# The S5 scan tile with sequence ahead of group, and x stored earlier through the Pool queue

## The chip, the cores and the metric

The kernel runs on one core of one Trainium2 chip. The metric is the device time of one execution in microseconds, as the median of several runs. The core has TensorE (PE, with its weight loads listed as PEld), VectorE (DVE), ScalarE (ACT), GpSimd (POOL) and SyncE (SP), which here only issues DMAs. ACT and POOL issue DMAs too, each in the order of its own program.

## What is computed

One inference step of a two-layer backbone for 128 prompt tokens and 128 sample tokens, D = 2048, all in float32. Layer 0 has attention, layer 1 an S5 state-space mixer; each is followed by a gated FFN. The change touches layer 1's mixer:

```python
def s5_mixer(h, h0_re, h0_im, w_in, a_re, a_im, log_dt, b_re, b_im, c_re, c_im, d_skip, w_gate, w_out):
    u = f32(h @ w_in)
    ug = u.reshape(bsz, length, N_GROUPS, GROUP_CH)          # 128 groups of 16 channels
    y = f32(d_skip) * u
    for d, rev in ((0, False), (1, True)):
        y_d, s_re, s_im = s5_direction(ug, ...)               # complex linear recurrence, 64 states a group
        y = y + y_d.reshape(bsz, length, D_MODEL)
    y = jax.nn.gelu(y).astype(h.dtype)
    y = y * jax.nn.sigmoid(y @ w_gate)
    return y @ w_out, ...
```

The kernel runs the recurrence over blocks of four positions: 32 steps in place of 128, forward on partitions 0 to 63 and backward on 64 to 127.

## The kernel before

The program is one long list of weight steps. Each loads 512 KB units into eight `raw` buffers (SP issues those loads in order, as buffers come free). Dense products are made from two float32r halves: for each unit ACT writes `whi` (L259 is the helper that records every ACT, DVE and POOL operation), DVE writes `wlo`, and PE runs 12 matmuls of 512 columns. L348 is the helper of all matmuls, L361 that of transposes. Beside the list run background tasks (generators); `pump` lets them emit their next piece when a planner, `Timeline`, thinks that its inputs are ready. The planner's costs (class `Timeline`, `engine`) thus set the order in which the engines' instructions are written; once written, each engine runs its own in order.

The mixer is worked in four quarters q of 32 groups, each in two halves e2 of 16:

- `w_in`: 32 units of dense products (8 for each q), whose result DVE transposes to `u(q)`. Layer norm tiles A6 to A9 are its left operand.
- `scan_task`: ACT masks `u` into `um` (two operations); PE multiplies it with a table into PSUM tiles `ms` (three banks in turn); ACT evacuates each 128x512 result in two halves of 64 partitions into the scan tile `SC` (16 operations of 64x512 for a quarter). The even quarters use tile S0, the odd ones tile X, which is also the tile that holds the activations x. So x is saved to DRAM (`xd`) first and read back at the end of the mixer.
- `steps_task`: the scan, 32 steps of four DVE operations of 128x128 on `SC`.
- `out_task`: ACT copies `SC` into two tiles `sf` (the layout copies, 64x2048, two for each e2); for each e2 PE runs 48 small matmuls (96 passes, in a trace 128x64) whose weights are slices of `sf` or of `u`; ACT applies gelu, PE transposes, ACT writes y. ACT also issues the loads of the next tables here: `cad` (CA, 1 MB) and four pieces `ld` (K, 128 KB each).
- `w_gate`: for each q 32 products of y(q) with raw weights (two passes of 512 columns each), which PE can only begin once y(q) is there. Quarter 3 is a dense product.

`SC` of quarter q + 2 reuses the tile of quarter q, and is written only after the layout copies of q have read it. In `SC`, element order is step, real/imaginary, group, batch: `[P, 33, 2, 32, 2]`. An evacuation and a layout copy then go through it with a distance of 128 elements (512 B) from one element to the next. The planner counts such an ACT operation as 2.15 times as long per element.

Of the kernel before, what the change touches and what calls it, by code (L numbers as in the profile page):

```python
# [11 lines left out]
AF = mybir.ActivationFunctionType  # L12
# [4 lines left out]
P = 128  # L17
# [52 lines left out]
class Timeline:  # L70
# [144 lines left out]
    def engine(self, eng, name, outs, ins, args, kw):  # L215
# [4 lines left out]
        if eng == "ACT":  # L220
            ps = self.in_psum(big[0])
            slow = 1.0
            for x in outs + big:
                st = [d for d in list(x.ap)[1:] if d[1] > 1]
                if st and abs(st[-1][0]) > 16: slow = 2.15
            c = (0.05 if ps else 0.095) + slow * n / 1200.0 + 0.09 * scal + 0.09 * ("accum_out" in kw)
            table = self.SETS.get(args[2], 0)
            if table and table != self.table:
                c, self.table = c + 1.29, table
        elif eng == "POOL":  # L230
            if name == "memset": c = 0.04 + n / 1200.0
# [57 lines left out]
def hybrid_kernel(ctx: ExitStack, tc: tile.TileContext, a):  # L289
# [1056 lines left out]
    class S5:  # L1346
# [25 lines left out]
        def u(self, q):  # L1372
            return self.uy[q // 2][:, q % 2]

        def load_T(self, e, h):
            (act_ if e else sync).dma_start(self.tT[:, h], Td[e][:, h])
# [13 lines left out]
        def scan_task(self):  # L1390
# [7 lines left out]
            self.kt = sb("A10", [P, 2048])  # L1398
            w1 = view(wt, 0, [[64, 2], [2, 32], [1, 2]])
            w2 = view(wt, 128, [[64, 2], [2, 32], [1, 2]])  # L1400
            for q in range(4):
                while not self.u_ready[q]:
                    yield
                while q > 1 and not self.sc_free[q - 2]:
                    yield
                if q == 1:
                    self.xd = dt("xd", [P, 2, D])
                    for b in range(2):
                        sync.dma_start(self.xd[:, b], x[b])
                um = sb("A2", [P, 16, 2, 2, 32])  # L1410
                SC = self.SC[q] = sb(("S0", "X")[q % 2], [P, 33, 2, 32, 2])
                u = self.u(q).rearrange("p (r n) -> p r n", n=64)
                for par in range(2):
                    act(um[:, :, par].rearrange("p r b c -> p r (b c)"), u, AF.Copy, scale=mask_par[:, par:par + 1])
                gps.memset(SC[:, 0, :, :, 0], 0.0)
                gps.tensor_copy(SC[:, 0, :, :, 1], s5par["H0"][:, :, 32 * q:32 * q + 32])
                for e2 in range(2):
                    e = 2 * q + e2
                    for h in range(2):
                        for ri in range(2):  # L1420
                            yield ready(um, tT[:, h], lag=S5_LAG, ahead=AHEAD)
                            bk = ms()
                            for i in range(4):
                                pr = e2 * 8 + h * 4 + i
                                mm(bk[:, i * P:(i + 1) * P], tT[:, h, i, ri],
                                   um[:, pr].rearrange("p a b c -> p (a b c)"), start=True, stop=True)
                            src = bk.rearrange("p (g c) -> p g c", c=32)
                            g0 = (e2 * 16 + h * 8) * 2
                            fw = view(SC, 128 + ri * 64 + g0, [[1, 16], [128, 32]], (0, 64))
                            bw = view(SC, 32 * 128 + ri * 64 + g0, [[1, 16], [-128, 32]], (64, 64))  # L1430
                            act(fw, src[0:64], AF.Copy)
# [3 lines left out]
                while self.scanned < q - 1:  # L1435
                    yield
                a_re = view(s5par["A4"], 32 * q, [[0, 2], [1, 32], [0, 2]])
                a_im = view(s5par["A4"], G + 32 * q, [[G, 2], [1, 32], [0, 2]])
                yield written(SC, lag=S5_LAG, ahead=AHEAD)
                self.scans.append((SC, a_re, a_im, w1, w2, q))  # L1440

        def steps_task(self):
            q = 0
            while q < 4:
# [3 lines left out]
                for s in range(32):  # L1448
                    cur = SC[:, s]
                    swp = view(SC, s * 128 + 64, [[-64, 2], [2, 32], [1, 2]])  # L1450
                    nxt = SC[:, s + 1]
# [9 lines left out]
        def out_task(self):  # L1461
# [8 lines left out]
            for q in range(4):  # L1470
# [4 lines left out]
                if q == 0:  # L1475
                    fin = view(sb("cw", [P, 4, 86]), 0, [[G, 2], [1, G]])
                gps.tensor_copy(fin[:, :, 32 * q:32 * q + 32], SC[:, 32, :, :, 0])
                sfs = [sb(t, [P, 2, 32, 32]) for t in ("A5", "A12")]
                for e2, sf in enumerate(sfs):
                    g0 = e2 * 32  # L1480
                    yield written(SC, lag=S5_LAG, ahead=AHEAD)
                    act(sf[0:64], view(SC, g0, [[64, 2], [1, 32], [128, 32]], (0, 64)), AF.Copy)
                    yield lambda now: tl.t["ACT"] < now + 2.0
                    act(sf[64:128], view(SC, 31 * 128 + g0, [[64, 2], [1, 32], [-128, 32]], (64, 64)), AF.Copy)
                self.sc_free[q] = True
                for e2, sf in enumerate(sfs):
# [3 lines left out]
                    for s in range(8):  # L1490
                        for ph in range(3):
                            for h in range(2):
                                g = h * 8 + s
                                o = bk[64 * h:64 * h + 64, 64 * s:64 * s + 64]
                                if ph < 2:
                                    mm(o, sf[:, ph, 2 * g:2 * g + 2].rearrange("p b c -> p (b c)"),
                                       ca[e % 2][:, g // 8, ph, :, g % 8], start=ph == 0, stop=False,
# [151 lines left out]
    s5 = S5()  # L1649
    m = s5.w_in()  # L1650
    start_hook(ffn0.last_up, lambda: (spawn(s5.steps_task()), spawn(s5.scan_task()), spawn(s5.out_task())))
    held, g1 = fill[-20:-16], fill[-16:]
# [109 lines left out]
```

## Time and profile before

| | us |
|---|---|
| median of three runs (lowest, highest) | 2644.32 (2640.66, 2646.99) |
| profiled execution, its own time | 2647.6 |
| its span | 2645.8 |
| PE busy in it | 2545.2 (96%) |
| DVE, ACT, POOL busy | 1599.1, 1323.0, 442.5 |

The profiled execution is 3.3 us above the median. The mixer lies between 1415 and 1900 us of the span; `w_in` ends at 1553, the dense part of `w_gate` begins at 1725. Most of the kernel is PE at work without a pause. In the stretch of the scans it is not: there PE has pauses of 2 to 14 us, and after them a lower granted clock.

### The profile page before, as it was taken

How to read it: one execution, taken by the hardware profiler on the slowest of the kernel's cores; microseconds unless marked ns; L12 is line 12 of the kernel's file. 1: busy time of each engine (PE TensorE's matmuls, PEld its weight loads, DVE VectorE, ACT ScalarE, POOL GpSimd, SP SyncE). 2: the span in 40 equal slices, each digit the busy share in tenths (PEclk: the TensorE clock that was granted, in tenths of full speed). 3: DMA queues.
4: the chain of work that ended last, by engine and by line, in shares of the span. 5: the costliest groups of instructions: out<-in, count | busy, mean ns of one | idle time of the engine just before them, and what ended most of it. 6: DMA issues, size and time to landing. Idle time of an engine off the chain costs nothing.

```text
span 2645.8 us, 35232 instructions
## 1 busy us (share of the span) xinstructions
PE 2545.2 (96%) x13011; PEld 1893.5 (72%) x13011; DVE 1599.1 (60%) x2370; ACT 1323.0 (50%) x1764; POOL 442.5 (17%) x455
## 2 busy tenths in 40 slices
PE   8999999999999999999998769999999999999998
PEld 4666677667777777777776655466677788888896
DVE  4765554567665665566656386655656565666566
ACT  5333444356554554455455668543555544554354
POOL 0002000011465555455530000000000000000000
PEclk9999999999999999999999889999999999999999
DMA  9979877977888888888886756789677756665663
GB/s 360 321 254 312 295 229 274 365 247 238 263 262 270 272 264 271 263 264 259 275 280 224 220 165 175 218 284 308 221 249 242 242 192 193 186 184 190 191 194 125
DMA packets 388741, 651.11 MB, mean 246 GB/s; under 512 B 81740, under 2 KB 100300, under 8 KB 386648
## 3 DMA queue, kind: packets, MB, share of 16 engines
q1 hardware_dynamic: 364064, 621.10, 71.5%
q10 hardware_dynamic: 20424, 20.47, 3.0%
q0 software_dynamic: 4080, 7.28, 0.9%
q8 instruction: 102, 1.67, 0.3%
q14 instruction: 71, 0.58, 0.1%
HBM read 623.72 MB, written 25.03 MB: 245 GB/s over the span
## 4 chain that ended last, share of the span: by engine, by line
PE 86%; ACT 4%; DVE 4%; DMA 3%; issue 1%; ACTq 1%; POOL 1%; SPq 0%
PE acc L348 73%; PE ada L348 6%; PE ms L361 4%; PE ms L348 3%; ACT A L259 2%; DVE A L259 2%; DVE wlo L259 1%; DMA raw<-in_ada_w_dram 1%; ACT X L259 1%; ACTq L259 1%; ACT whi L259 1%; DMA raw<-in_na_w_o_dram 1%; POOL S L259 1%; ACT S L259 0%; DMA xd<-X 0%
## 5 line engine op out<-in xcount | busy, mean ns | idle before, releaser
L348 PE MATMUL acc<-whi,A 128*128 128x512 f32 (+1 forms) x5536 | 1796.7, 396 | 31.2 <-ACT whi L259 22.4
L259 DVE TENSOR_TENSOR wlo<-raw,whi 128x1024 fp32r<-128x1024 f32 (+2 forms) x697 | 885.8, 1276 | 688.5 <-ACT whi L259 668.8
L348 PEld LDWEIGHTS acc<-whi,A 128*128 128x128 f32 x5536 | 1042.8, 189 | 358.6 <-issue 92.5
L348 PE MATMUL acc<-wlo,A 128*128 128x512 f32 (+1 forms) x2768 | 1080.6, 390 | 11.4 <-DVE wlo L259 10.9
L259 ACT ACTIVATE whi<-raw 128x1024 fp32r<-128x1024 f32 (+2 forms) x697 | 724.5, 1043 | 693.2 <-PE acc L348 557.5
L348 PEld LDWEIGHTS acc<-wlo,A 128*128 128x128 f32 x2768 | 523.2, 189 | 117.7 <-DVE wlo L259 21.0
L259 DVE SCALAR_TENSOR_TENSOR A<-ms,cw,A 128x254 f32<-128x254 f32 x344 | 157.8, 479 | 88.9 <-ACT A L259 80.6
L348 PE MATMUL ada<-raw,cond 128*32 128x512 f32 (+1 forms) x1396 | 196.9, 595 | 6.1 <-DVE adaev L259 4.0
L259 POOL TENSOR_TENSOR S<-S,A 128x512 f32<-128x512 f32 x128 | 182.8, 1448 | 50.3 <-PE ms L361 50.3
L259 POOL DMA_DIRECT2D adab<-in_ada_b_dram x48 | 24.9, 518 | 711.5 <-DVE ada L259 383.6
L259 POOL TENSOR_TENSOR S<-S 128x512 f32<-128x512 f32 (+1 forms) x96 | 132.9, 1384 | 7.5
L259 ACT ACTIVATE A<-ms,cw 128x256 f32<-128x256 f32 x172 | 88.0, 562 | 87.9 <-PE ms L361 87.9
L361 PEld LDWEIGHTS ms<-ident,A 128*128 128x128 f32 (+2 forms) x670 | 80.5, 142 | 47.4 <-ACT A L259 16.2
L361 PE MATMUL ms<-ident,A 128*128 128x128 f32 (+2 forms) x670 | 101.5, 277 | 11.0 <-ACT A L259 10.1
L259 ACT ACTIVATE A<-A 128x512 fp32r<-128x512 f32 (+7 forms) x88 | 72.1, 824 | 66.1 <-DVE A L259 65.5
L259 ACT ACTIVATE A<-ms 128x512 f32<-128x512 f32 (+3 forms) x106 | 55.1, 558 | 96.1 <-PE ms L348 51.0
L348 PE MATMUL ms<-A,A 128*64 128x64 f32 (+1 forms) x1152 | 79.7, 253 | 23.4 <-ACT A L259 19.6
L348 PEld LDWEIGHTS ms<-A,A 128*64 128x64 f32 (+1 forms) x1152 | 75.8, 168 | 35.8 <-ACT A L259 24.2
L259 ACT ACTIVATE S<-ms 128x128 f32<-128x128 f32 (+2 forms) x96 | 58.4, 644 | 70.2 <-PE ms L361 64.5
L348 PE MATMUL acc<-raw,A 128*128 128x512 f32 x192 | 89.3, 614 | 4.3 <-ACT A L259 4.3
L259 ACT ACTIVATE A<-acc 128x512 f32<-128x512 f32 (+1 forms) x112 | 65.2, 588 | 50.4 <-PE acc L348 50.3
L259 POOL DMA_DIRECT2D A<-in_final_g_dram x1 | 0.6, 555 | 504.4 <-ACT whi L259 504.4
(138 smaller groups left out, 1499.0 us busy)
## 6 DMA issues: line engine op xcount, KB each, us to landing
raw<-in_ada_w_dram SPq DMA_DIRECT2D x331, 512.0 KB
raw<-in_ffn_w_up_dram SPq DMA_DIRECT2D x318, 512.0 KB
raw<-in_ffn_w_down_dram SPq DMA_DIRECT2D x168, 512.0 KB
raw<-in_na_w_qkv_dram SPq DMA_DIRECT2D x71, 512.0 KB
raw<-in_s_w_in_dram SPq DMA_DIRECT2D x32, 512.0 KB
raw<-in_s_w_gate_dram SPq DMA_DIRECT2D x32, 512.0 KB
raw<-in_s_w_out_dram SPq DMA_DIRECT2D x32, 512.0 KB
raw<-in_na_w_o_dram SPq DMA_DIRECT2D x28, 512.0 KB
```

Of the source, the lines that this page charges most:

```text
L259: return fn(*args, **kw)
L348: nc.tensor.matmul(out, lhsT, rhs, **kw)
L361: nc.tensor.transpose(out, in_, ident[:n, :n])
```

## The change

Five things are edited:

1. `SC` becomes `[P, 33, 2, 2, 32]`: step, real/imaginary, batch, group. The scan's views follow; its operations stay 128x128.
2. An evacuation writes runs of 8 adjacent elements and reads PSUM with a distance of 64 elements; there are still 16 of 64x512 for a quarter.
3. A layout copy becomes two of 64x1024, each read and written in runs of 8. The tile `sf` gets group innermost, 8 wide, so the weights of 32 of the 48 small matmuls are now read with a distance of 8 elements (32 B).
4. x is stored to DRAM by POOL at the second step of `w_in`, not by SP ahead of quarter 1.
5. The planner no longer counts a distance in PSUM as slow. With this and the shorter runs its orders change on all engines; a pause between the two halves of a layout copy is dropped.

```diff
-                if st and abs(st[-1][0]) > 16: slow = 2.15
+                if st and abs(st[-1][0]) > 16 and not self.in_psum(x): slow = 2.15
...
+        def keep_x(self):
+            self.xd = dt("xd", [P, 2, D])
+            for b in range(2):
+                gps.dma_start(self.xd[:, b], x[b])
...
-                if q == 1:
-                    self.xd = dt("xd", [P, 2, D])
-                    for b in range(2):
-                        sync.dma_start(self.xd[:, b], x[b])
...
-                SC = self.SC[q] = sb(("S0", "X")[q % 2], [P, 33, 2, 32, 2])
+                SC = self.SC[q] = sb(("S0", "X")[q % 2], [P, 33, 2, 2, 32])
...
-                            src = bk.rearrange("p (g c) -> p g c", c=32)
-                            g0 = (e2 * 16 + h * 8) * 2
-                            fw = view(SC, 128 + ri * 64 + g0, [[1, 16], [128, 32]], (0, 64))
-                            bw = view(SC, 32 * 128 + ri * 64 + g0, [[1, 16], [-128, 32]], (64, 64))
+                            src = bk.rearrange("p (g b c) -> p c b g", b=2, c=32)
+                            g0 = e2 * 16 + h * 8
+                            fw = view(SC, 128 + ri * 64 + g0, [[128, 32], [32, 2], [1, 8]], (0, 64))
+                            bw = view(SC, 32 * 128 + ri * 64 + g0, [[-128, 32], [32, 2], [1, 8]], (64, 64))
...
-                sfs = [sb(t, [P, 2, 32, 32]) for t in ("A5", "A12")]
+                sfs = [sb(t, [P, 2, 2, 64, 8]) for t in ("A5", "A12")]
...
-                    act(sf[0:64], view(SC, g0, [[64, 2], [1, 32], [128, 32]], (0, 64)), AF.Copy)
-                    yield lambda now: tl.t["ACT"] < now + 2.0
-                    act(sf[64:128], view(SC, 31 * 128 + g0, [[64, 2], [1, 32], [-128, 32]], (64, 64)), AF.Copy)
+                    for h in range(2):
+                        g0 = e2 * 16 + h * 8
+                        to = sf[:, h].rearrange("p i (b c) g -> p i b c g", b=2)
+                        act(to[0:64], view(SC, g0, [[64, 2], [32, 2], [128, 32], [1, 8]], (0, 64)), AF.Copy)
+                        act(to[64:128], view(SC, 31 * 128 + g0, [[64, 2], [32, 2], [-128, 32], [1, 8]], (64, 64)), AF.Copy)
...
-                                    mm(o, sf[:, ph, 2 * g:2 * g + 2].rearrange("p b c -> p (b c)"),
+                                    mm(o, sf[:, h, ph, :, s],
...
+    start_hook(m[1], s5.keep_x)
```

On DVE, at the end of `w_in`, the order before is as follows (`S_2131` is quarter 0's scan tile, the pair of transposes is `w_in`'s last).

```order
L259 TENSOR_TENSOR wlo_12675<-raw_12420,whi_12674 128x1024
...
L259 TENSOR_TENSOR A_2128_12042<-S_2131_12045,A4t_4707 128x128 x2
L259 TENSOR_TENSOR S_2131_12045<-S_2131_12045,A_2128_12042 128x128 x2
L259 STREAM_TRANSPOSE A_2127_12033<-acc_2209_12548 128x16x32
L259 STREAM_TRANSPOSE A_2127_12033<-acc_2210_12549 128x16x32
L259 TENSOR_TENSOR A_2128_12042<-S_2131_12045,A4t_4707 128x128 x2
L259 TENSOR_TENSOR S_2131_12045<-S_2131_12045,A_2128_12042 128x128 x2
```

After, in the same place (`X_12268` is quarter 1's scan tile):

```order
L259 TENSOR_TENSOR wlo_12697<-raw_12465,whi_12696 128x1024
L259 TENSOR_TENSOR wlo_12715<-raw_12514,whi_12714 128x1024
L259 TENSOR_TENSOR A_2128_12045<-X_12268,A4t_4707 128x128 x2
L259 TENSOR_TENSOR X_12268<-X_12268,A_2128_12045 128x128 x2
...
L259 STREAM_TRANSPOSE A_2127_12036<-acc_2209_12592 128x16x32
L259 STREAM_TRANSPOSE A_2127_12036<-acc_2210_12593 128x16x32
L259 TENSOR_TENSOR A_2128_12045<-X_12268,A4t_4707 128x128 x2
```

Before, five of quarter 0's 32 steps stand behind the last transposes, and its scan begins two `wlo` after the second pair of transposes; now it begins right behind that pair, all 32 steps stand ahead of the last two `wlo`, and seven steps of quarter 1 ahead of the last transposes.

On ACT, behind `w_in`'s last `whi`, before (`A_2230` and `A_2231` are the tiles `sf`, `A_2234` is `um` of quarter 2):

```order
L259 ACTIVATE whi_12674<-raw_12420 128x1024
L259 DMA A_2226_12746<-cad_125 128x2048
L259 ACTIVATE A_2230_12771<-S_2131_12045 64x2048 x2
L259 ACTIVATE A_2231_12772<-S_2131_12045 64x2048 x2
L259 ACT_TABLE_LOAD
L259 ACTIVATE A_2128_12042<-ms_12833 128x8x4x16
...
L259 DMA A_2129_12043<-ld_135 32x16x64 x4
L259 ACTIVATE A_2126_12032<-ms_12987 128x256 x2
L259 ACTIVATE S_2235_12902<-ms_12994 64x16x32 x2
```

And after (`A_2231` is now `um`):

```order
L259 ACTIVATE whi_12714<-raw_12514 128x1024
L259 DMA A_2226_12790<-cad_125 128x2048
L259 ACTIVATE A_2228_12794<-S_2131_12048 64x1024 x4
L259 ACTIVATE A_2229_12795<-S_2131_12048 64x1024 x4
L259 ACTIVATE A_2231_12813<-A_2127_12036,maskpar_70 128x16x64 x2
...
L259 DMA A_2129_12046<-ld_135 32x16x64 x4
L259 ACTIVATE S_2232_12814<-ms_12975 64x32x2x8 x2
L259 ACTIVATE S_2232_12814<-ms_12982 64x32x2x8 x2
L259 DMA A_1939_10985<-td_121 128x1024
L259 ACTIVATE A_2126_12035<-ms_12990 128x256 x2
```

The load of `cad` still stands ahead of the layout copies; `um` of quarter 2 has moved ahead of the gelu, and four evacuations of quarter 2 ahead of the first y.

On POOL the two stores of x stand ahead of quarter 0's first scan writes, with nothing between the last bias loads and them:

```order
L259 DMA adab_80<-in_ada_b_dram 2x512 x2
L259 DMA xd<-X_89 128x2048 x2
L259 MEMSET S_2131_12048 128x2x32
L259 COPY S_2131_12048<-H_942_4708 128x2x32
L259 MEMSET X_12268 128x2x32
```

Before, SP had them between the eleventh and the twelfth of the last sixteen `w_in` loads. On PE, the list of matmuls is the same; ahead of the small matmuls of quarter 1 stand 20 of quarter 0's 32 gate products where there were 32, ahead of those of quarter 2 stand 42 gate products in all where there were 56, and ahead of those of quarter 3 there are 72 where there were 90.

## Rows read from the trace of the kernel before

**Rows 1.** The page's first part: busy us (share of the span), instructions.

```profile
PE 2545.2 (96%) x13011; PEld 1893.5 (72%) x13011; DVE 1599.1 (60%) x2370; ACT 1323.0 (50%) x1764; POOL 442.5 (17%) x455
```

**Rows 2.** Busy us by engine in a slice, then granted clock, DMA share, GB/s.

```profile
1560.00:1580.00 20.00, 8.54 (x180) 8.41 (x182) 18.73 (x77) 18.86 (x8) 0.70 (x3) 0.61 0.36 91
```

**Rows 3.** Timeline of PE: start, us, instruction, count, [idle before <- what ended it].

```profile
1512.75 0.80 PE L348 MATMUL acc<-whi,A 128*128 128x512 f32 x1 [6.84 <-ACT whi L259]
...
1568.53 4.71 PE L348 MATMUL ms<-A,A 128*64 128x64 f32 x96 [14.17 <-ACT A L259]
...
1585.62 3.27 PE L348 MATMUL acc<-raw,A 128*128 128x512 f32 x4
...
1602.96 17.33 PE L348 MATMUL acc<-raw,A 128*128 128x512 f32 x40
...
1665.66 3.02 PE L348 MATMUL ms<-A,A 128*64 128x64 f32 x96
...
1685.06 12.19 PE L348 MATMUL acc<-raw,A 128*128 128x512 f32 x24 [4.34 <-ACT A L259]
```

**Rows 4.** Timeline of ACT (ACTq: DMAs that it issues), same columns.

```profile
1415.83 2.94 ACT L259 ACTIVATE whi<-raw 128x1024 fp32r<-128x1024 f32 x3
...
1430.52 1.04 ACT L259 ACTIVATE whi<-raw 128x1024 fp32r<-128x1024 f32 x1
...
1505.43 1.03 ACT L259 ACTIVATE X<-ms 64x512 f32<-64x512 f32 x1 [7.89 <-DMA xd<-X]
...
1553.41 0.33 ACTq L259 DMA_DIRECT2D A<-cad  x1
1561.03 15.09 ACT L259 ACTIVATE A<-S 64x2048 f32<-64x2048 f32 x4 [15.99 <-DVE S L259]
...
1580.95 3.42 ACTq L259 DMA_DIRECT2D A<-ld  x4
...
1674.06 10.52 ACTq L259 DMA_DIRECT2D A<-ld  x4
```

**Rows 5.** Timeline of DVE, same columns.

```profile
1492.11 1.31 DVE L259 STREAM_TRANSPOSE A<-acc 128x512 f32<-128x512 f32 x2
...
1561.91 0.49 DVE L259 TENSOR_TENSOR A<-X,A4t 128x128 f32<-128x128 f32 x2
...
1595.63 0.53 DVE L259 TENSOR_TENSOR A<-S,A4t 128x128 f32<-128x128 f32 x2
1610.93 0.62 DVE L259 TENSOR_TENSOR S<-S,A 128x128 f32<-128x128 f32 x2 [14.76 <-ACT S L259]
```

**Rows 6.** ACT's groups by shape: count | busy us, mean ns of one | idle.

```profile
L259 ACT ACTIVATE A<-acc 128x512 f32<-128x512 f32 x104 | 61.4, 596 | 48.4 <-PE acc L348 48.3
...
L259 ACT ACTIVATE X<-ms 64x512 f32<-64x512 f32 x32 | 33.9, 1059 | 19.8 <-PE ms L348 7.9 <-DMA xd<-X 7.9 <-issue 3.6
L259 ACT ACTIVATE S<-S 64x384 f32<-64x384 f32 x64 | 33.0, 516 | 5.0 <-POOL S L259 4.6
...
L259 ACT ACTIVATE A<-S 64x2048 f32<-64x2048 f32 x8 | 30.2, 3780 | 16.1 <-DVE S L259 16.0
...
L259 ACT ACTIVATE A<-A 128x1024 f32<-128x1024 f32 x20 | 21.1, 1054 | 5.1 <-DVE A L259 5.1
...
L259 ACT ACTIVATE A<-ms 128x256 f32<-128x256 f32 x16 | 5.2, 383 | 16.0 <-DMA A<-ld 10.4 <-issue 3.2 <-PE ms L361 1.5
```

**Rows 7.** Chain of work that ended last: start, us, what; prices of PE's pieces.

```profile
1480.87 2.76 PE acc L348 x12
1483.63 1.78 PE ms L348 x16
```

**Rows 8.** Groups by shape, 1440 to 1760 us: `wlo`, and PEld's small weights.

```profile
L259 DVE TENSOR_TENSOR wlo<-raw,whi 128x1024 fp32r<-128x1024 f32 x35 | 42.2, 1221 | 63.8 <-ACT whi L259 56.8 <-DMA A<-td 6.8
...
L348 PEld LDWEIGHTS ms<-A,A 128*64 128x64 f32 x768 | 26.1, 152 | 24.2 <-ACT A L259 21.2 <-issue 2.3 <-ACT whi L259 0.8
```

**Rows 9.** The slice (columns as rows 2) in which x becomes final.

```profile
1415.00:1425.00 10.00, 7.27 (x32) 5.78 (x33) 7.74 (x13) 6.32 (x11) 0.00 (x0) 0.83 1.01 360
```

More of the change, by code (lines that the diff above doesn't have):

```diff
@@ L1398, in scan_task @@
             self.kt = sb("A10", [P, 2048])
-            w1 = view(wt, 0, [[64, 2], [2, 32], [1, 2]])
-            w2 = view(wt, 128, [[64, 2], [2, 32], [1, 2]])
+            w1 = view(wt, 0, [[64, 2], [32, 2], [1, 32]])
+            w2 = view(wt, 128, [[64, 2], [32, 2], [1, 32]])
             for q in range(4):
@@ L1414, in scan_task @@
                     act(um[:, :, par].rearrange("p r b c -> p r (b c)"), u, AF.Copy, scale=mask_par[:, par:par + 1])
-                gps.memset(SC[:, 0, :, :, 0], 0.0)
-                gps.tensor_copy(SC[:, 0, :, :, 1], s5par["H0"][:, :, 32 * q:32 * q + 32])
+                gps.memset(SC[:, 0, :, 0], 0.0)
+                gps.tensor_copy(SC[:, 0, :, 1], s5par["H0"][:, :, 32 * q:32 * q + 32])
                 for e2 in range(2):
@@ L1436, in scan_task @@
                     yield
-                a_re = view(s5par["A4"], 32 * q, [[0, 2], [1, 32], [0, 2]])
-                a_im = view(s5par["A4"], G + 32 * q, [[G, 2], [1, 32], [0, 2]])
+                a_re = view(s5par["A4"], 32 * q, [[0, 2], [0, 2], [1, 32]])
+                a_im = view(s5par["A4"], G + 32 * q, [[G, 2], [0, 2], [1, 32]])
                 yield written(SC, lag=S5_LAG, ahead=AHEAD)
@@ L1449, in steps_task @@
                     cur = SC[:, s]
-                    swp = view(SC, s * 128 + 64, [[-64, 2], [2, 32], [1, 2]])
+                    swp = view(SC, s * 128 + 64, [[-64, 2], [32, 2], [1, 32]])
                     nxt = SC[:, s + 1]
@@ L1476, in out_task @@
                     fin = view(sb("cw", [P, 4, 86]), 0, [[G, 2], [1, G]])
-                gps.tensor_copy(fin[:, :, 32 * q:32 * q + 32], SC[:, 32, :, :, 0])
-                sfs = [sb(t, [P, 2, 32, 32]) for t in ("A5", "A12")]
+                gps.tensor_copy(fin[:, :, 32 * q:32 * q + 32], SC[:, 32, :, 0])
+                sfs = [sb(t, [P, 2, 2, 64, 8]) for t in ("A5", "A12")]
                 for e2, sf in enumerate(sfs):
-                    g0 = e2 * 32
                     yield written(SC, lag=S5_LAG, ahead=AHEAD)
-                    act(sf[0:64], view(SC, g0, [[64, 2], [1, 32], [128, 32]], (0, 64)), AF.Copy)
-                    yield lambda now: tl.t["ACT"] < now + 2.0
-                    act(sf[64:128], view(SC, 31 * 128 + g0, [[64, 2], [1, 32], [-128, 32]], (64, 64)), AF.Copy)
+                    for h in range(2):
[3 more added lines that the diff above has]
+                        act(to[64:128], view(SC, 31 * 128 + g0, [[64, 2], [32, 2], [-128, 32], [1, 8]], (64, 64)), AF.Copy)
                 self.sc_free[q] = True
```

## The prediction, made before the changed kernel had run

> **What bounds the kernel now.** I read the page's busy times first: PE is busy for 2545 us, 96% of the span [rows 1], so the kernel is PE's list of matmuls plus PE's pauses, and a change that leaves the list alone can win only pauses and low-clock stretches. Next came the table of slices, to find them: in the slice at 1560 PE is busy for 8.5 of 20 us, at a granted clock of 0.61 of full speed, while ACT is busy for 18.9 and DVE for 18.7 [rows 2]. Then PE's timeline, for the pauses themselves: 6.84 us at 1506, 14.17 us at 1554, 4.34 us at 1681, all ended by ACT [rows 3]. Then ACT's, for what it was waiting on or doing at those times: the first time it waited for x to reach DRAM, the second time it ran four layout copies in 15.09 us after waiting for the scan [rows 4]. Last DVE's: the scans of quarters 0 and 1 follow one another without a pause (1561.9 to 1595.6, so 33.7 us for 32 steps), but quarter 2's waits 14.76 us for ACT's evacuations [rows 5]. So in the scans' stretch a ring bounds the time: ACT's copies free the scan tile, ACT's evacuations fill it, DVE scans, ACT copies, and PE waits for the result.
>
> **Prices of the edits on ACT.** An evacuation of 64x512 takes 1.059 us, against 0.596 for 512 elements that lie in a row; a copy of 64x2048 takes 3.780, against two of 1024 adjacent elements at 1.054 each [rows 6]. Both are about twice as slow per element. With runs of 8 the price lies between these. The nearest row is the copy with runs of 16, 0.516 us for 384 elements, which on the slope of the plain rows is the full rate [rows 6]; I take 0.60 and 1.05, and no gain at all as the other end. The new reading of PSUM with a distance of 64 elements has a near row too: y is read from PSUM with a distance of 128, and its 256 elements take 0.383, so 0.213 less than 512 adjacent ones, 0.83 ns for each [rows 6]; no extra price. ACT's work falls by 64 x 0.46 = 29.6 us and by 60.5 - 32 x 1.05 = 26.9 us, 56 in all. How much of it reaches the end has to be walked through, on PE's clock. Scan operations keep their size; I take 1.054 us for a step, as before.
>
> **The store of x.** It leaves SP's queue, where only weight loads were behind it, and PE's pause of 6.84 us [rows 3] goes with ACT's wait of 7.89 [rows 4]. On POOL two issues stand ahead of quarter 0's first scan writes, which are needed 80 us later. x is final at about 1413, and the DMA share just then is 1.01 [rows 9]: its 2 MB at 360 GB/s take 5.8 us from the weight loads. The cover is that ACT's `whi` has three units at 1415.8 and wants the next at 1430.5 only [rows 4]. Without that cover it would cost 5.8.
>
> **`w_in`.** From its second transposes (1492.1 [rows 5]) to its end (ACT's `cad` follows it at 1553.4 [rows 4]) are 61 us. PE's work there is 16 units of 2.76 and four times 1.78 of evacuation matmuls [rows 7], 51 us; the rest is the pause and its clock. Once the pause is gone DVE is next: by its new order it has 32 scan steps (33.7), 14 `wlo` of 1.22 [rows 8] and a pair of transposes (1.3) ahead of the last unit, so 52.1 after 1493.4, then 2.76 of PE: the end comes at 1548.3, **5.1 us earlier**. Quarter 0's scan ends before that (about 1543) where it ended at 1561.9.
>
> **The pause at 1554.** The copies cannot start before `w_in` has ended, since ACT issues `cad` ahead of them and that load overwrites the last norm tile; so the earlier scan end buys nothing more. Four copies of 1.05 later, at 1552.7 in place of 1568.5 [rows 3], PE starts the small matmuls: PE waits some 3.5 us where it waited 14.17. **Another 10.7 us.**
>
> **To gate quarter 0** (before: 17.1 us from 1568.5 to 1585.6 [rows 3]). The steps stay: 96 passes at low clock (4.71), 96 more, four K issues on ACT (3.42 [rows 4]), two pieces of y (0.7). Now 4 evacuations (2.4) stand ahead of y, but the copies, which held the second half up, are done before the first half's passes are. 4.7 + 4.7 + 3.4 + 2.4 + 0.7 = 15.9: **1.2 us.**
>
> **Gate quarter 0 to the small matmuls of quarter 2** (before: 80.0 us, 1585.6 to 1665.7 [rows 3]). At 0.433 us a pass (17.33 for 40 [rows 3]) and 0.111 for an evacuation pass [rows 7], PE's work there was 112 gate passes, 112 evacuation passes and 7.8 of other work, 68.7 us; 11.3 were lost. After: 84 gate passes, 104 evacuation passes and 6.8, 54.7. What is lost is walked through thus, from a start at 1568.6. Quarter 2's evacuations end at 1589.3 (PE gives their last matmuls at 1587, ACT adds 2.4); quarter 1's copies follow, so its small matmuls start at 1593.8, PE 2 us late. The scan of quarter 2 runs 1589.4 to 1623.2. Behind the copies ACT has masks, gelu, K issues; PE, out of PSUM banks, waits some 2.8. Quarter 3's evacuations end at 1625.6, quarter 2's copies free PE at 1630, 1.6 late. That is 61.4 us, 6.7 lost in place of 11.3: **4.6 us.** The scan of quarter 3 ends near 1665.
>
> **The rest.** From quarter 2's small matmuls to quarter 3's PE lost 6 us, the 4.34 and its clock (24 passes in 12.19 where 10.4 would do [rows 3]), because ACT took 10.52 us for four K issues [rows 4]. I leave that loss in. Quarter 3's scan and first copies are then done before PE has reached them. PE carries 18 gate products (15.6 us) past that point, which now cover quarter 3's gelu and transposes. I let nothing more come of the shorter tail, and later stages merely shift.
>
> Sum: 5.1 + 10.7 + 1.2 + 4.6 = **21.6 us**. The profiled execution of before took 2647.6 (its span and 1.8 around it, which the change does not touch), 3.3 above the median of 2644.3; so 2626 in its terms, 2623 in the median's.
>
> **An edit that may cost.** The weights of 64 of each 96 small passes are now read with a distance of 32 bytes. No row shows such a load. The passes come every 31 ns (3.02 for 96 [rows 3]), while a load is listed with 152 ns of overlapping time [rows 8]. The lower end is nothing, the load hidden; the nearest row of a strided read is the copy on ACT, twice as slow per element. If the loads set the 31 ns and double, 512 passes lose 31 each, 16 us. The forecast takes nothing, since loads of 152 ns in passes of 31 already run beside other matmuls; the range takes the rest. [...]
>
> **Rivals.**
> - *Weight loads double* and set the pace: 21.6 - 16 leaves 5.6 us, 2639. For: ACT's strided reads double. Against: the overlap.
> - *Weight loads four times as long*: 512 x 93 ns = 48 us, on PE, whose list has no slack there: 26 us slower, 2671. The point from which this decides is 42 ns added to a pass (21.6 us / 512). For: 152 ns listed for a load leaves little to hide it in if the pairs of passes have to wait for each other. Against: ACT's doubling is the worst ratio in the trace.
> - *K issues stall more often.* ACT's four issues took 3.42 us once and 10.52 another time [rows 4]; the same number now falls into a shorter time, and everything on ACT's ring waits behind. Each further long one costs 7 us; two or three eat the gain up: 2637 to 2644, about no change.
> - *Runs of 8 give half*: 0.23 more for an evacuation, 0.42 for a copy. That is 1.7 us before the first small matmuls and some 3 in each of two turns of the ring: 8 us less, 2631.
> - *The store of x collides* with the loads at 1415: 5.8 less, 2629. It cannot simply fail to help: 80 us lie between it and the first write of tile X.
>
> **Chances.** Forecast 0.44 (2613 to 2631), weight loads double 0.18, K stalls 0.15, runs of 8 half or x colliding 0.13, weight loads far slower or another loss beyond 5 us 0.10. 0.2% is 5.3 us, about what a measurement can tell. Faster: 0.44 + 0.13 and about half of the two middle rivals, 0.72. Same: the other half, 0.16. Slower: 0.12 with a little of the stalls. The range reaches from 2608, should the long K issue vanish too and the tail give something, to 2646, the case of three K stalls.
>
> **What would show it.** Evacuations at 0.6 and copies at 1.05 us; no wait for `xd`; PE's pause after `w_in` at 3 to 4 us; the three later scans without a gap of over 10 us between quarters 1 and 2 and of over 3 between 2 and 3; 96 small passes in 3.0 us at full clock. 4.5 us or more there would mean that the weights cost. K issues of over 10 us more than once would be the third rival.

## The result and the profile after

The changed kernel takes 2631.14 us (median of 6 runs, 2627.21 to 2634.14) against 2644.52 for the kernel before beside it: a ratio of 0.9948, with a 95% interval from 0.9934 to 0.9962, so 13.8 us faster (10.0 to 17.5). The forecast was 2623. The time lies in the range, and 8 us beyond the forecast, on the way to the rival in which the weight loads double.

The profiled execution has a span of 2632.4 us, 13.4 less than before's 2645.8. The first part of its page (busy us, share of the span, instructions) answers [rows 1]:

```profile
PE 2555.5 (97%) x13011; PEld 1904.6 (72%) x13011; DVE 1599.2 (61%) x2370; ACT 1267.4 (48%) x1780; POOL 445.2 (17%) x457
```

ACT lost 55.6 us of work; the prediction counted 56. PE, whose list has not changed, is busy 10.3 us *longer*. What is left of the span when PE's busy time is taken away, its pauses, falls from 100.6 to 76.9 us. So 23.7 us of pauses were won, near the forecast's sum of 21.6 (which counts time at the lower clock too), and 10.3 were given back inside PE's own work. The groups of instructions by shape between 1440 and 1760 us (count | busy us, mean ns of one | idle before them) show both sides, beside [rows 6, 8]:

```profile
L259 ACT ACTIVATE X<-ms 64x512 f32<-64x512 f32 x32 | 18.9, 592 | 10.9 <-PE ms L348 10.5
L259 ACT ACTIVATE A<-S 64x1024 f32<-64x1024 f32 x16 | 16.9, 1056 | 8.6 <-DVE X L259 8.3
L348 PEld LDWEIGHTS ms<-A,A 128*64 128x64 f32 x768 | 40.1, 192 | 9.9 <-ACT A L259 6.1 <-issue 3.8
```

The evacuations take 0.592 us (0.60 predicted), the copies 1.056 (1.05). The small matmuls' weight loads went from 152 to 192 ns on the mean of all 768, and two thirds of those are the strided ones. PE's timeline (start, us, instruction, count, [idle before <- what ended it]) follows; it answers [rows 3]:

```profile
1519.69 0.50 PE L348 MATMUL acc<-wlo,A 128*128 128x512 f32 x1 [1.13 <-DVE wlo L259]
...
1544.15 1.06 PE L348 MATMUL ada<-raw,cond 128*32 128x512 f32 x8
1546.86 0.46 PE L348 MATMUL ms<-A,A 128*64 128x64 f32 x2 [1.64 <-ACT A L259]
1549.01 12.09 PE L348 MATMUL ms<-A,A 128*64 128x64 f32 x206 [1.69 <-ACT A L259]
...
1566.94 3.02 PE L348 MATMUL acc<-raw,A 128*128 128x512 f32 x4
...
1597.45 4.99 PE L348 MATMUL ms<-A,A 128*64 128x64 f32 x96
...
1614.19 1.11 PE L361 MATMUL ms<-ident,A 128*128 128x128 f32 x4 [7.15 <-ACT X L259]
...
1638.08 0.45 PE L348 MATMUL ms<-A,A 128*64 128x64 f32 x2
...
1713.67 0.50 PE L348 MATMUL acc<-whi,S 128*128 128x512 f32 x1
```

The pause of 6.84 us in `w_in` is gone, that of 14.17 has become 1.64 and 1.69, and the one of 4.34 near 1681 is gone too. A new one stands at 1607, 7.15 us. And 96 small passes take 4.99 us where they took 3.02: 1.97 more, 15.8 for the eight groups of 96 if all of them run at the full clock. ACT's timeline (ACTq: DMAs that it issues) tells where the new pause comes from:

```profile
1602.95 8.98 ACTq L259 DMA_DIRECT2D A<-ld  x4
1611.97 0.60 ACT L259 ACTIVATE A<-acc 128x512 f32<-128x512 f32 x1 [8.82 <-issue]
...
1651.23 9.92 ACTq L259 DMA_DIRECT2D A<-ld  x4
```

ACT stands 9 us at four K issues, with the evacuations that PE needs queued behind them. It is what took 10.52 us in [rows 4], once in a place where PE has nothing else to do (1603), once where gate products cover it (1651). Below it is called the K stall, and the section on the K issues shows what ACT waits for.

### The profile page after: what moved, and what is told of

Same layout as the page of the kernel before. It is cut to its first block, busy times and chain, and to the rows that moved or that the text cites. A ratio compares the mean times of both kernels' runs of the same rounds, so it can differ in the third digit from the quotient of the medians.

```text
span 2632.4 us, 35245 instructions
## 1 busy us (share of the span) xinstructions
PE 2555.5 (97%) x13011; PEld 1904.6 (72%) x13011; DVE 1599.2 (61%) x2370; ACT 1267.4 (48%) x1780; POOL 445.2 (17%) x457
## 4 chain that ended last, share of the span: by engine, by line
PE 87%; DVE 5%; DMA 3%; ACT 3%; issue 1%; POOL 1%; ACTq 0%; SPq 0%; POOLq 0%; DVEq 0%
PE acc L348 73%; PE ada L348 6%; PE ms L348 4%; PE ms L361 4%; DVE A L259 2%; DVE wlo L259 2%; ACT A L259 2%; DMA raw<-in_na_w_o_dram 1%; DMA raw<-in_na_w_qkv_dram 1%; ACT whi L259 1%; DMA raw<-in_ada_w_dram 1%; POOL S L259 1%; DVE S L259 0%; ACTq L259 0%; DVE X L259 0%
## 5 line engine op out<-in xcount | busy, mean ns | idle before, releaser
L259 POOL TENSOR_TENSOR S<-S,A 128x512 f32<-128x512 f32 x128 | 181.9, 1440 | 52.1 <-PE ms L361 52.1
L361 PEld LDWEIGHTS ms<-ident,A 128*128 128x128 f32 (+2 forms) x670 | 81.2, 143 | 52.1 <-issue 13.4
L348 PEld LDWEIGHTS ms<-A,A 128*64 128x64 f32 (+1 forms) x1152 | 88.9, 194 | 20.5 <-ACT A L259 9.2
L348 PE MATMUL ms<-A,A 128*64 128x64 f32 (+1 forms) x1152 | 92.6, 272 | 7.0 <-ACT A L259 4.0
L348 PEld LDWEIGHTS ada<-raw,cond 128*32 128x32 f32 x1396 | 32.1, 109 | 74.0 <-issue 55.6
```

Of the source, the lines that this page charges most:

```text
L259: return fn(*args, **kw)
L348: nc.tensor.matmul(out, lhsT, rhs, **kw)
L361: nc.tensor.transpose(out, in_, ident[:n, :n])
```

## Experiments

Each kernel was timed beside the kernel before. The figures below are its ratio to that kernel, with the 95% interval, and that ratio times 2644.5 in microseconds. By the intervals, a difference between two kernels is uncertain by some 6 us. Spans, pauses and single times are those of one profiled execution each.

### The strided weights: `dense_w`, `old_far_w`

```diff
-                                    mm(o, sf[:, h, ph, :, s],
+                                    mm(o, sf[:, h, ph, 8 * s:8 * s + 8].rearrange("p n g -> p (n g)"),
```

> The changed kernel with one edit: the small matmuls read 64 adjacent elements as weights in place of 64 that lie 32 bytes apart. The elements are the wrong ones, so the mixer's sums are wrong; count, sizes and order of all instructions stay. Theory 1 (the distance costs 31 ns for each of 512 passes and all of it is on PE's path): 96 small passes in 3.0 us in place of 4.99, the whole 12 to 16 us faster than the changed kernel, 2615 to 2619. Theory 2 (the passes are quicker but ACT's ring of copies, evacuations and K issues sets the end there): 3.0 us for 96 passes, but PE waits longer elsewhere, 2626 to 2631. Theory 3 (the passes became slower for another reason than the distance): 4.99 us for 96, 2631.

Ratio 0.9908 (0.9892 to 0.9924), 2620: 10.6 us faster than the changed kernel, and within 3 us of the forecast, which counted nothing for the weights. PE's timeline, ACT's timeline and the first part of its page follow:

```profile
1563.44 2.08 PE L348 MATMUL ms<-A,A 128*128 128x128 f32 x8 [4.88 <-ACT S L259]
...
1595.23 3.02 PE L348 MATMUL ms<-A,A 128*64 128x64 f32 x96
...
1612.51 1.12 PE L361 MATMUL ms<-ident,A 128*128 128x128 f32 x4 [9.67 <-ACT X L259]
```

```profile
1600.22 10.03 ACTq L259 DMA_DIRECT2D A<-ld  x4
```

```profile
PE 2540.7 (97%) x13011; PEld 1890.2 (72%) x13011; DVE 1599.3 (61%) x2370; ACT 1267.0 (48%) x1780; POOL 443.7 (17%) x457
```

The distance is the cause of the 31 ns per pass: with it gone, 96 passes take 3.02 us again and PE is busy 14.8 us less. But its pauses grow from 76.9 to 84.2 us (span 2624.9), since PE comes earlier to waits that ACT ends: 9.67 us in place of 7.15 at the K stall, 4.88 in place of 2.92 ahead of gate quarter 0. Theory 1 holds for the price. Theory 2 holds for a part of what it brings: a third of 15.8 by the ratios, half by the profiled executions. The time lies between the ranges of the two.

`old_far_w` puts the same distance, alone, into the kernel before:

```diff
-                                    mm(o, sf[:, ph, 2 * g:2 * g + 2].rearrange("p b c -> p (b c)"),
+                                    mm(o, view(sf, ph * 1024 + (g // 8) * 512 + g % 8, [[8, 64]]),
```

> The kernel before with one edit: the weights of the small matmuls are read 32 bytes apart (the wrong elements, so the mixer's sums are wrong; all else stays). Theory 1 (the distance costs 1.97 us for 96 passes, all on PE's path): 12 to 16 us slower than before, 2656 to 2660. Theory 2 (a part of it lies in the pauses in which PE waits for ACT's copies, as the 6 to 10 us that the adjacent weights gave in the new layout say): 5 to 10 us slower, 2649 to 2654. Theory 3 (the old ring hides all of it): 2644 to 2647.

1.0025 (1.0016 to 1.0035), 6.6 us slower, as theory 2 has it. PE's timeline, at the lower clock and at the full one:

```profile
1564.91 5.47 PE L348 MATMUL ms<-A,A 128*64 128x64 f32 x96 [14.18 <-ACT A L259]
...
1615.47 5.00 PE L348 MATMUL ms<-A,A 128*64 128x64 f32 x96
```

PE is busy 10.6 us longer, and its pauses are 5.4 us shorter (95.2 for 100.6), so a part of the price lies in time in which PE waited anyway. Another part is the clock: after the pause of 14 us, at a granted clock of 0.59 (0.60 in the same passes of before), the 96 passes take 5.47 us where they took 4.71, 0.76 more and not 1.97.

### The store of x: `x_only`, `late_x`

`x_only` is the kernel before with the move of the store alone:

```diff
-                    for b in range(2):
-                        sync.dma_start(self.xd[:, b], x[b])
...
+    start_hook(m[1], s5.keep_x)
```

> The kernel before with one edit: the store of x is issued by POOL at the second w_in step; the scan tile, the evacuations and the copies stay as they were. Theory 1 (PE's pause of 6.84 us at 1506 and its clock go, nothing else does): w_in ends 5 to 9 us earlier, the four copies of 3.78 us still stand between its end and the first small matmuls, every later pause stays; 2635 to 2640 us, evacuations 1.06, copies 3.78, 96 small passes 3.0 us. Theory 2 (the scan's ring takes the gain back, because scan 0 ends only 8 us after w_in does): w_in ends earlier but the small matmuls start as late as before; 2643 to 2645. Theory 3 (the gain of w_in belongs wholly to the store): w_in's end at 1544, as in the changed kernel.

0.9961 (0.9948 to 0.9973), 10.3 us faster. PE's timeline has no pause over 0.4 us in `w_in` after 1465, and then:

```profile
1542.26 1.07 PE L348 MATMUL ada<-raw,cond 128*32 128x512 f32 x8
1558.60 5.16 PE L348 MATMUL ms<-A,A 128*64 128x64 f32 x96 [15.27 <-ACT A L259]
```

As theory 1 says, if a little more: `w_in` ends earlier and everything shifts. In the old layout the store is worth 10 us. `late_x` takes it back in the new one:

```diff
-    start_hook(m[1], s5.keep_x)
...
+                if q == 1:
+                    self.xd = dt("xd", [P, 2, D])
+                    for b in range(2):
+                        sync.dma_start(self.xd[:, b], x[b])
```

> The changed kernel with one edit undone: x is stored where it was, by SP ahead of quarter 1's first scan writes. Theory 1 (the early store is worth the pause of 6.84 us and its clock, as x_only's 10 us against before say): ACT waits for xd again, PE stands some 7 us in w_in, 2638 to 2642. Theory 2 (the shorter evacuations let the wait start and end earlier, since scan 0 begins earlier): 2633 to 2636. Theory 3 (the store is worth nothing in the new layout): 2631.

0.9909 (0.9893 to 0.9926): 24.1 us faster than before, and 10.3 faster than the changed kernel, against all three theories. Two readings explain it. First, SP's timeline of the kernel before (upper fence) and of `late_x` (lower), at the store:

```profile
1464.67 30.25 SPq L259 DMA_DIRECT2D raw<-in_s_w_in_dram  x11
1494.97 0.93 SPq L259 DMA_DIRECT2D xd<-X  x2
```

```profile
1461.24 13.47 SPq L259 DMA_DIRECT2D raw<-in_s_w_in_dram  x6
1474.76 0.93 SPq L259 DMA_DIRECT2D xd<-X  x2
```

The planner now counts quarter 0's evacuations as cheap, emits quarter 1 sooner, and so writes the store behind 6 loads in place of 11. Each of them waits on SP for a free buffer. The store starts 20 us earlier and nobody waits for it: with the new layout and its order the wait goes without the early store. (No run has the planner's edit without the layout.) Second, ACT's K issues in the same kernel:

```profile
1601.90 3.35 ACTq L259 DMA_DIRECT2D A<-ld  x4
```

3.35 us in place of 8.98. PE's pause before the transposes there is 0.45 us in place of 7.15:

```profile
1609.58 0.66 PE L361 MATMUL ms<-ident,A 128*128 128x128 f32 x4 [0.45 <-ACT A L259]
```

### The K issues: `k_pool`, `late_x_kp`, `k_first`

```diff
             for j in range(4):
-                act_.dma_start(
+                gps.dma_start(
                     view(self.kt, (e % 2) * 1024, [[64, 16], [1, 64]], (32 * j, 32)),
```

> The changed kernel with one edit: the four DMA issues for each K come from POOL's queue in place of ACT's. Theory 1 (the 9 us that ACT stood at the K issues at 1603 are a delay of its own queue, and PE's pause of 7.15 us at 1607 comes of it alone): no stretch over 2 us without work on ACT there, the pause shrinks to under 2 us, PE is not thrown to its lower clock; 2622 to 2626. Theory 2 (the issues wait for the DMA engines, whoever issues): POOL stands instead, K lands as late, PE waits for K in place of ACT; 2629 to 2633. Theory 3 (POOL makes the pieces of 256 bytes itself, slowly): the issues take POOL far longer than ACT's 3 us for four, the first K are late too; over 2634.

0.9865 (0.9850 to 0.9880): 2609, 22 us faster than the changed kernel. POOL's timeline at the same place, and the page's first part:

```profile
1587.02 2.57 POOL L259 DMA_DIRECT2D A<-ld  x4 [3.82 <-PE ms L348]
```

```profile
PE 2546.2 (98%) x13011; PEld 1901.3 (73%) x13011; DVE 1601.5 (61%) x2370; ACT 1267.4 (49%) x1780; POOL 465.3 (18%) x489
```

Each of POOL's 32 issues takes 0.65 us, none more than 0.69. From 1495 to 1720 PE has no pause over 1.7 us, and with the pauses went much of its time at the lower clock. Over 1545 to 1700 the granted clock (third figure from the end) is 0.94 in the changed kernel and 0.99 here:

```profile
1545.00:1700.00 155.00, 140.67 (x1125) 91.95 (x1122) 100.30 (x382) 73.17 (x102) 1.65 (x7) 0.94 0.63 178
1545.00:1700.00 155.00, 154.90 (x1146) 99.07 (x1143) 98.08 (x352) 73.43 (x105) 19.80 (x36) 0.99 0.68 209
```

In the whole span PE is busy 9.3 us less. Theory 1 is right about the cause, but 2609 is below its range, since both places where ACT stood contribute: `w_in` ends at 1536.8 in place of 1544.2 (the wait of 5.97 us behind the first eight K issues, at 1463, is gone), and the dense part of the gate begins at 1690.3 in place of 1713.7. Part of this may be the planner's, which prices an issue differently on the two queues.

`late_x_kp` is `late_x` with this edit.

> late_x (the changed kernel with x stored as before) with the K issues from POOL's queue. late_x came out 10 us faster than the changed kernel, against all three expectations; its trace shows no wait for xd and 3.35 us for the four K issues at 1602 where the changed kernel's took 8.98. Theory 1 (in the new layout the early store of x buys nothing, and the 10 us are the K stall that this kernel's times happen to avoid): without K on ACT the two kernels are alike, 2609 to 2614, as k_pool (2611). Theory 2 (the early store costs 10 us by itself, by its transfer beside the weight loads): 2600 to 2604. Theory 3 (the late store has a price that the stall hid): 2616 to 2620.

0.9860 (0.9843 to 0.9876), 2607.5 against k_pool's 2609: alike within the uncertainty. So theory 1: in the new layout the early store brings nothing that these runs can tell, and the 10 us between `late_x` and the changed kernel were in the main the K stall. Their profiled executions agree: from gate quarter 0 to the dense part of the gate `late_x` takes 136.9 us and the changed kernel 146.7.

`k_first` asks what ACT stands for, with the two lines of the issues exchanged:

```diff
-                        ca[e % 2] = self.load_CA(e + 2)
                         self.load_K(e + 2)
+                        ca[e % 2] = self.load_CA(e + 2)
```

> The changed kernel with one edit: in each half quarter the four K issues stand ahead of the issue of the 1 MB of CA on ACT's queue, in place of behind it. Theory 1 (the K issues stand because the queue still works at the megabyte in front of them): four K issues in 3 to 4 us each time, PE's pause of 7.15 us at 1607 shrinks to under 2, 2620 to 2625. Theory 2 (they stand because of the pieces of K themselves, 512 of 256 bytes in each issue, of this K and the one before it): 9 us stay, 2629 to 2633; the wait may then move on to the CA issue behind them.

0.9935 (0.9920 to 0.9950): 2627, alike with the changed kernel within the uncertainty, between the two theories' ranges. ACT's four issues of quarters 1 and 2, then PE's pause:

```profile
1599.76 7.00 ACTq L259 DMA_DIRECT2D A<-ld  x4
...
1645.79 4.68 ACTq L259 DMA_DIRECT2D A<-ld  x4
```

```profile
1609.69 1.12 PE L361 MATMUL ms<-ident,A 128*128 128x128 f32 x4 [5.48 <-ACT X L259]
```

They are shorter than 8.98 and 9.92, but they stand without the megabyte of CA in front of them. Nor were the DMA engines full: the stretch of the changed kernel in which ACT stood has a DMA share of 0.75, where 1.15 is reached elsewhere (busy us of PE, PEld, DVE, ACT, POOL, then granted clock, DMA share, GB/s):

```profile
1602.90:1611.90 9.00, 4.14 (x28) 3.22 (x26) 8.45 (x35) 0.25 (x1) 0.00 (x0) 0.90 0.75 206
...
1651.20:1661.10 9.90, 9.90 (x33) 4.19 (x33) 9.35 (x37) 0.23 (x1) 0.00 (x0) 1.00 1.15 273
```

What ACT waits for stands in the traces. The row of 8.98 us merges four issues that take 0.55, 0.73, 0.55 and 0.64 us; 6.44 us lie between the second and the third. The chain of work that ended last (start, us, what) names the end of that wait, here for the changed kernel at 1604 and for the kernel before at 1676:

```profile
1604.39 6.29 DMA raw<-in_ada_w_dram
1610.68 0.02 issue
1610.70 0.55 ACTq L259
```

```profile
1675.88 7.45 DMA raw<-in_ada_w_dram
1683.33 0.02 issue
1683.35 0.55 ACTq L259
```

ACT waits until a weight load that SP issued has landed. The traces list for each DMA of this program a semaphore, and on it the time of the landing. In them a K issue starts only after the DMA before it on the same semaphore has landed, 0.02 us after it at the least. The issues of SP and ACT share eight semaphores (100 to 105, 115 and 116 in the traces of before and of the changed kernel), POOL's use eight others (106 to 113). In the eight traces with K on ACT there are 15 waits of over 1.2 us in front of a K issue. Each ends 20 to 22 ns before the issue starts, with the last landing report of the DMA before it on that semaphore: ten times a load of SP, five times one of ACT. In `k_first` too the third issue of quarter 1 waits for a load of SP, 4.55 us. On POOL, whose semaphores SP's loads do not use, the last landing lay 23 us or more behind each K issue that came after a pause. So at 1603 neither the pieces of K nor the megabyte of CA in front of them make the K stall, but the load that used the semaphore before. At 1651 it is two K issues of ACT (of 1646.40 and 1651.23) that had not landed yet. The first eight K issues, at 1450, are another case: there a single issue takes up to 4.67 us in the changed kernel, and why stays open.

### The layout when K is off ACT: `old_k_pool`, `kp_dense_w`

`old_k_pool` is `x_only` with K's issues on POOL; `kp_dense_w` is `dense_w` with them.

> The kernel before with two edits: x is stored by POOL at the second w_in step, and the K issues come from POOL's queue; the scan tile, evacuations, copies and weights are those of before. It is k_pool (2611 us) without the new layout, so the difference of the two is what the layout is worth when no K issue stands on ACT. Theory 1 (the layout's gain and its strided weights nearly cancel, 16.5 against 15.8): 2609 to 2614. Theory 2 (the layout's shorter pauses are worth some 9 us net, as x_only and the changed kernel differ by 4 to 5 and a K stall of 7 lay in the changed kernel alone): 2618 to 2622. Theory 3 (the whole 16.5 shows and the weights lie in shadow): 2626 to 2629. Under all three the pause at w_in's start (5.5 us) and the one of 5.9 us at 1676 go, evacuations stay at 1.06 and copies at 3.78.

> k_pool with the weights read adjacent (the wrong elements, so the mixer's sums are wrong; count, sizes and order of instructions stay). With K on ACT the same edit gave 10.5 of 15.8 us, and PE's pause at the K issues grew by 2.5. Theory 1 (the missing part went into the K stall, PE's list is the bound otherwise): the whole 15.8 come, 2594 to 2598. Theory 2 (a part of the strided loads lies in waits for the scan or the copies whichever queue issues K): 2600 to 2604. Theory 3: the ring of ACT and DVE is the bound, 2606 or more.

`old_k_pool`: 0.9894 (0.9879 to 0.9909), 7.7 us slower than `k_pool`. So the layout is worth 8 us net when K is off ACT, with an uncertainty of 6: nearest to theory 2, just below its range, and theory 1 is not excluded. In `old_k_pool` the four copies still hold PE for 11.05 us after `w_in`:

```profile
1547.81 5.12 PE L348 MATMUL ms<-A,A 128*64 128x64 f32 x96 [11.05 <-ACT A L259]
```

`kp_dense_w`: 0.9842 (0.9827 to 0.9857), 6 us faster than `k_pool`, where theory 1 wanted 15.8. PE is busy 14.4 us less, but its pauses grow from 64.4 to 68.9, waits for the table `td` of 5.8 us among them. That makes 9.9 between the two profiled executions, of which `k_pool`'s is its slowest and `kp_dense_w`'s its fastest; the ratios give 6. Theory 2 or 3, the interval does not part them.

### Can the weights be had cheaper: `dense_sf`, `kp_runs4`, `kp_runs2`

`dense_sf` makes the copies write adjacent weights:

```diff
-                sfs = [sb(t, [P, 2, 2, 64, 8]) for t in ("A5", "A12")]
+                sfs = [sb(t, [P, 2, 2, 8, 64]) for t in ("A5", "A12")]
...
-                        to = sf[:, h].rearrange("p i (b c) g -> p i b c g", b=2)
+                        to = sf[:, h].rearrange("p i g (b c) -> p i b c g", b=2)
...
-                                    mm(o, sf[:, h, ph, :, s],
+                                    mm(o, sf[:, h, ph, s],
```

> The changed kernel with one edit, and the full computation: the copies write the weights so that the 64 of a group are adjacent, so the matmuls read them without distance, while the copies read runs of 8 and write single elements 256 bytes apart. Theory 1 (ACT pays for a distance on the side of the write as on that of the read): copies of 1.9 to 2.0 us in place of 1.056, ACT carries 27 to 30 us more, PE 15.8 less; the pause after w_in grows from 3.3 to 7 us and the ring loses some 3 us in each of its turns; 2619 to 2627. Theory 2 (a distance costs ACT only when it reads): copies of 1.05, 2615 to 2618, the best of all. Theory 3 (PE's list does not count, ACT's does): slower than the changed kernel, over 2634.

1.0005 (0.9996 to 1.0014): the whole gain is gone. The copies, by shape:

```profile
L259 ACT ACTIVATE A<-S 64x1024 f32<-64x1024 f32 x16 | 32.2, 2014 | 12.2 <-DVE X L259 8.3 <-DVE S L259 3.6
```

2.0 us, so ACT pays for this distance on the write (2014 ns for 1024 elements) as before's copies did for theirs on the read (3780 for 2048 [rows 6]): theory 1 for the price, theory 3 for the time. The PE passes are quick (3.0 us for 96 at the full clock), and PE waits: its pauses are back at 100.5 us. Of these, 7.0 us stand behind the copies after `w_in`, where it was 3.3, and 13.4 in two pauses behind K issues (1623 and 1676), where it was 7.15 in one. So both the ring of copies, evacuations and scan and the K stall took the gain. No run parts them, since this layout was not run with K on POOL.

`kp_runs4` and `kp_runs2` have K on POOL and `sf` as `[P, 2, 2, 8/r, 64, r]` with r = 4 and 2. For r = 2:

```diff
+                        for i in range(2):
+                            to = [[2, 64], [128, 4], [1, 2]]
+                            at = h * 1024 + i * 512
+                            act(view(sf, at, to, (0, 64)), view(SC, i * 64 + g0, [[32, 2], [128, 32], [1, 8]], (0, 64)), AF.Copy)
...
+                                    mm(o, sf[:, h, ph, s // 2, :, s % 2],
```

> k_pool with the full computation, and the copies' output in runs of 4 elements, so that the 64 weights of a group lie 16 bytes apart in place of 32; 64 copies of 64x512 in place of 32 of 64x1024. [...] Theory 2 (the price goes with the distance in bytes): about 4.0 us for 96 passes, some 8 us less, 2603 to 2607. Theory 3 (runs of 4 are too short for ACT): copies near 1.0 us, over 2615.

> kp_runs4 with runs of 2, so that the 64 weights of a group lie 8 bytes apart, two in each 16 bytes; full computation. At 16 bytes the 96 small passes took 4.93 us, as at 32 (4.99). Theory 1 (a weight load pays for each 16 bytes it touches): half as many, so 96 passes in about 4.0 us, midway between 4.93 and 3.02. Theory 2 (every distance costs the same): 4.9. For ACT's copies with runs of 2: 0.63 us if 8 bytes in a row are enough, up to 1.0 if 16 are wanted. 2608 to 2613 with theory 1 and quick copies, 2612 to 2620 else.

PE's 96 small passes and ACT's copies, first with runs of 4, then of 2:

```profile
1575.04 4.93 PE L348 MATMUL ms<-A,A 128*64 128x64 f32 x96
```

```profile
L259 ACT ACTIVATE A<-S 64x512 f32<-64x512 f32 x32 | 20.1, 629 | 15.2 <-PE acc L348 8.8 <-DVE S L259 5.9
```

```profile
1573.37 3.15 PE L348 MATMUL ms<-A,A 128*64 128x64 f32 x96
```

```profile
L259 ACT ACTIVATE A<-S 64x512 f32<-64x512 f32 x32 | 21.3, 665 | 18.0 <-PE acc L348 8.9 <-DVE S L259 8.6
```

At 16 bytes the weights cost what they cost at 32 (4.93 us for 96 passes, against 4.99), where theory 2 of `kp_runs4` wanted 4.0; at 8 bytes they cost nearly nothing (3.15, against 3.02): neither the 4.0 nor the 4.9 of `kp_runs2`'s theories. `kp_runs4`: 0.9891 (0.9876 to 0.9907), 2616, by the ratios 7 us slower than `k_pool`. It has 6.4 us more of copies, but that these make the difference is not shown: the two profiled executions are 0.6 us apart, with pauses of 64.4 us each. `kp_runs2`: 0.9842 (0.9828 to 0.9857), 2603, below both of its ranges. It does the full computation, gives as much as `kp_dense_w` does with the weights adjacent, and no kernel here is faster: 42 us under before, 28 under the changed kernel.

## Why the prediction was right, and where it was not

**Prices on ACT**: right to 1%; "runs of 8 give half" fell.

**The store of x**: the waits went as said (7.89 on ACT, 6.84 on PE), and the store's transfer at 1413 collided with nothing (PE waits 2.63 us for `whi` there, before and after). But the step credited the wrong edit. With the new layout and its order the wait goes without it (`late_x`, `late_x_kp`); by itself, in the old layout, the store is worth 10 us (`x_only`). The prediction took the old place of the store on SP as given.

**`w_in`**: 9.2 us earlier, not 5.1. Of this 3.0 was won before quarter 1's transposes, the second pair, where the walk begins:

```profile
1489.10 1.30 DVE L259 STREAM_TRANSPOSE A<-acc 128x512 f32<-128x512 f32 x2
```

It was 1492.11 before [rows 5]. The walk from there came out 6.1 us shorter, near the 5.1. The 3.0 may be quarter 0's cheaper evacuations, which the walk left out, but `x_only`, which does not have them, reaches that point 2.4 us early as well; the profiled executions differ by as much ahead of it.

**The pause at 1554**: 3.3 us for 3.5. **To gate quarter 0**: 17.9 us from 1549.0, not 15.9. The strided weights stand in this stretch, but they are not the miss: in `dense_w` it takes 18.3 us (from 1548.5 to 1566.8), with 4.88 us of waiting for ACT's evacuations. ACT's work between the passes and the gate sets it, the K issues among it; with K on POOL it takes 14.6 us (`k_pool`), and 11.7 with adjacent weights as well (`kp_dense_w`).

**Gate quarter 0 to the small matmuls of quarter 2**: 71.1 us, not 61.4. The K stall (7.15 us, and the lower clock after it, 0.50 from 1615 to 1619: four passes in 3.62 us there, where 1.88 is usual) and quarter 1's weights (3.9) are more than the miss. This is the third rival, once, at the 7 us that it was priced with. But its reason was another: the prediction read ACT's 10.52 us [rows 4] as the price of four issues in a shorter time, and the trace of before has 8.06 of them as the wait for a load of SP. In `late_x` quarter 1's issues have no such wait.

**The rest**: the loss of 4.34 us that was left in did not come. ACT stood 9.92 us at 1651, much as before, but PE now had gate products in reserve.

**The weights** are the step that failed: "The forecast takes nothing, since loads of 152 ns in passes of 31 already run beside other matmuls". The overlap with other matmuls did not hide the strided loads here, where each of the 768 passes has a load of its own. 96 passes take 4.99 us in place of 3.02, and nothing but the loads' distance differs in `dense_w`. Put down to the 64 strided ones, that is an estimate of 62 ns for such a pass in place of 31, the "double" end of the bound; it cost 14.8 us of PE. Whether the adjacent loads already set the 31 ns, or only keep up with it, no run shows. The rival of four times as long fell: a strided pass grew by 31 ns, not by 93, and stayed under the 42 from which it would have decided. What was sized wrong in the other direction is the rival's 2639: PE's list does have slack in this stretch, so the distance cost 6 to 11 us at the end, each uncertain by 6 or less (`old_far_w` 6.6, `kp_dense_w` 6, `dense_w` 10.6).

The sum without the weights was 21.6, and `dense_w` measures 24.3. Inside it two gains that the forecast did not have (4.1 us more in `w_in`, and the 4.34 us of loss that did not come) nearly cancel with a K stall (7.15 us in the changed kernel, 9.67 in `dense_w`) and the clock after it. That 21.6 came out so well is in part luck: in the 15 waits above a K issue stood until the DMA that used its semaphore before had landed, and the change moved which DMA that was without aiming at it.

## What to carry to other kernels

A layout has a reader on each engine: price the change on all of them before the sum is made, and where a row of many short instructions shows a steady pace, ask what a slower load of an operand would do to it (here 4.99 us for 96 passes in place of 3.02). A DMA issue stands in the program of the engine that issues it, and here ten of ACT's 15 long waits at K issues were for the landing of a load of SP; a merged row of issues hides that, so look at the single issues and at what each waits for. When such a wait lasts 6 to 10 us, as here (6.44 in the changed kernel, 9.62 in `x_only`), try the issue on an engine for which nobody waits and which does not share the semaphore: here that was worth 22 us (`k_pool`). And an edit that makes a planner's costs smaller moves the other edits' operations too, so each edit's worth has to be measured with and without the others: here 10 us, nothing, or a loss for the same store.

## What the runs showed of the hardware

- 96 passes with 128x64 float32 weights, 64 of them with weights 4, 8, 16 or 32 bytes apart, take 3.02, 3.15, 4.93 and 4.99 us at the full clock (`dense_w`, `kp_runs2`, `kp_runs4`, the changed kernel). At 16 and 32 bytes that is 30 and 31 ns more for each of the 64, so about 62 ns where a pass at 4 bytes takes 31 (an estimate, from those times). No run tells why.
- At a granted clock of 0.59 to 0.60 the distance of 32 bytes cost 0.76 us for such 96 passes (5.47 in place of 4.71), at the full clock 1.97.
- ACT writes runs of 8, 4 and 2 float32 at 1.056 (of 1024 elements), 0.629 and 0.665 us (of 512); single elements 256 bytes apart cost twice, 2.0 us for 1024. It reads PSUM 256 bytes apart at 0.592 us for 512, as fast as in a row (0.596 [rows 6]).
- An issue of 512 pieces of 256 bytes took ACT 0.55 to 0.73 us in the K stall and POOL 0.65 to 0.69. From the start of the first to the end of the fourth it was 2.6 to 12 us on ACT (12.07 in `x_only`, 9.62 of it one wait for a load of SP). On POOL it was 2.6 us, and 4.4 for one group of each kernel. In `k_pool` K landed a median of 7.1 us after POOL's issue.
